# Score products of two attention mixers: low keys padded to 128 rows, and 64-row products moved behind the 128-row ones

## The chip, the cores and the metric

The kernel runs on one core of a Trainium2 chip (trn2). The metric is the device time of one execution in microseconds (us). Of the core's engines the text speaks of TensorE (PE: matrix products; its loads of the stationary operand have a row of their own, PEld), VectorE (DVE), ScalarE (ACT), GpSimd (POOL) and the queue that starts most transfers (SP). TensorE computes with a stationary operand that it loads first and a moving operand that it streams. The result goes to PSUM, from where DVE and ACT read it. A product "with 128 rows" contracts over all 128 partitions, one "with 64 rows" over half of them.

## The reference

A decoder trunk of two layers, sequence 512, width 1024. Each layer is a channel mixing (SwiGLU), a token mixer, and another channel mixing. The token mixer of layer 0 is a convolution beside sparse attention, that of layer 1 a short convolution beside stick-breaking attention. What the change touches are the scores, queries times keys, of eight heads of 64 in either mixer:

```python
def _nsa(q, kc, vc, ks, vs, kw, vw, gates, ...):          # layer 0
    ...
        s_s = jnp.einsum('bqgrd,bgqnd->bqgrn', qg, k_sel).astype(jnp.float32) * scale
        ...
        s_w = jnp.einsum('bqgrd,bsgd->bqgrs', qg, kwb).astype(jnp.float32) * scale
        ...
        o = gq[..., 0:1] * o_c + gq[..., 1:2] * o_s + gq[..., 2:3] * o_w

def _stick_breaking(q, k, v):                             # layer 1
    ...
        z = jnp.einsum('bqhd,bshd->bhqs', qb, k).astype(jnp.float32) * scale
        ...
        log_a = jax.nn.log_sigmoid(z) + lax.cumsum(log_keep, axis=3, reverse=True) - log_keep
```

In layer 0 the selected and the window branch both cover all earlier tokens here (sequence 512, window 512, all blocks selected), so that each head has two full causal score matrices.

## The kernel before

**Precision.** Every operand is kept as a high part and a low part (`split`, lines L93 and L94: ACT rounds, DVE subtracts), and a product is the sum of high times high, high times low and low times high. A head has 64 features, half of the 128 partitions. So a query tile holds the high part in one half of the partitions and the low part in the other half, and a key tile holds the high keys twice. One product with 128 rows then gives (high + low query) times high key. What is missing, high query times low key, is a second product with 64 rows that uses only the half with the high query.

**First mixer** (`mixer0`, layer 0). After the projections, L735 to L764 do the compressed branch. The loop over eight heads (in the order 0, 4, 1, 5, ...) and two branches follows: for four blocks `i` of 128 queries a score tile `ss` with (i+1)*128 columns is computed by L815 (128 rows, stationary `qst`, moving `kt_`) and L816 (64 rows, the same stationary columns, moving `klo`). DVE adds the bias and takes the extremum (L818), ACT takes the exponential (L820), POOL scales by the gate (L825), PE transposes (L487, ten blocks for one head and branch), ACT and DVE split what comes out (`th`, `tl`, L93 and L94), and PE weighs the values (L497, L498). At the end of a head L830 and L831 add the compressed branch (32 rows), and ACT and DVE join the halves (L477, L478). A convolution of one channel block runs on PE (`cv`, L123 to L125) and that of three others on DVE (`cc`, L559), both as filling work with a late priority. `klo` is two tiles, one for each branch: its lower 64 partitions belong to key group 0, its upper ones to key group 1.

**Second mixer** (`mixer1`, layer 1). For each of eight heads a tile `z` of three PSUM banks takes, for the blocks 3, 2, 0, 1, a product with 128 rows (L912), one with 64 rows (L913) and the causal mask as a product with the identity (L916, L919). Two sigmoids of ACT read the whole `z` (L922, L925), DVE makes the running product (L929, L930), then come transposes and weighing as in the first mixer. The projections of the short convolution (`ac`, L123 to L125, through `short_conv`) fill PE with a late priority. There is one `z` buffer.

**Order.** The instructions of each engine are put in a fixed order by a list scheduler when the program is built: by a priority that follows the order of the code, lowered for what stands under `later()`, and by its own estimate of times. On the chip each engine runs its list in order and waits by semaphores. Buffers are rotating pools; of the tags that matter here the first mixer has three `ss`, two `pt` and two `po` banks of PSUM.

Of the kernel before, what the change touches and what calls it, by code (L numbers as in the profile page):

```python
# [7 lines left out]
F32 = mybir.dt.float32  # L8
# [3 lines left out]
ALU = mybir.AluOpType  # L12
AX = mybir.AxisListType

P = 128
T = 512
# [14 lines left out]
OFFQ = [896, 1024, 512, 0]  # L31
# [24 lines left out]
def trunk(ctx: ExitStack, tc: tile.TileContext, a: dict, out: bass.AP):  # L56
    nc = tc.nc
    V, S, G, PE = nc.vector, nc.scalar, nc.gpsimd, nc.tensor
# [27 lines left out]
    ident_r = const.tile([P, P], F32R, name="ident_r")  # L86
    mask_r = const.tile([P, P], F32R, name="mask_r")
# [423 lines left out]
    def mixer0(norm, nxt, ph):  # L511
# [52 lines left out]
        qst = [qb[h // 3][:, (h % 3) * T:(h % 3 + 1) * T] for h in range(NH)]  # L564
# [107 lines left out]
        for n in (3, 3, 2):  # L672
            hi, lo = load_w(a["ab_v"][:, k * 280:(k + n) * 280], n * 280)
            for j in range(n):
                sl = slice(j * 280, (j + 1) * 280)
                for i in range(NT):
                    ts = slice(i * P, (i + 1) * P)
                    o = pvs[i][:, :280]
# [14 lines left out]

        kb = [ph.rtile("kst", "q", 1536) for _ in range(2)]
        kb = [b[:, i * T:(i + 1) * T] for b in kb for i in range(3)]
        kt_, klo = kb[:4], kb[4:]
        for br in range(2):
            pk = alt()
            proj(norm, a["ab_a"][10 + br], pk)
            kk = ctile("kk")  # L700
            V.tensor_tensor(kk, pk, rstd, ALU.mult)
            for g in range(2):
                r, r2 = slice(g * 64, g * 64 + 64), slice(64 - g * 64, 128 - g * 64)
                kg = kt_[2 * g + br]
                S.activation(kg[r, :], kk[r, :], AF.Copy)
                S.activation(kg[r2, :], kk[r, :], AF.Copy)
                V.tensor_tensor(klo[br][r, :], kk[r, :], kg[r, :], ALU.subtract)

        for j in range(4):
            pq = alt()  # L710
# [3 lines left out]
            for g in range(2):  # L714
                r, r2 = slice(g * 64, g * 64 + 64), slice(64 - g * 64, 128 - g * 64)
                q = qst[j + 4 * g]
# [55 lines left out]
        with later():  # L772
# [19 lines left out]
            for j in range(4):  # L792
                z = conv[j]
# [9 lines left out]
        for n, h in enumerate([0, 4, 1, 5, 2, 6, 3, 7]):  # L803
            g, hh, slope = h // 4, h % 4, 2.0 ** -(h + 1)
            rg = slice(g * 64, g * 64 + 64)
            po = pbt("po", "po")
            kw = dict(skip_group_check=True)
            for br in range(2):
                p_ = ph.tile("pp", "p", 1281)
                st = sm.tile([P, 8], F32, tag="st", name=nm("st"))  # L810
                for i in range(NT):
                    w = (i + 1) * P
                    ts = slice(i * P, (i + 1) * P)
                    ps = pbt("ss")
                    PE.matmul(ps[:, :w], qst[h][:, ts], kt_[2 * g + br][:, :w], start=True, stop=False)  # L815
                    PE.matmul(ps[:, :w], qst[h][rg, ts], klo[br][rg, :w], start=False, stop=True)  # L816
                    e = p_[:, OFFQ[i]:OFFQ[i] + w]
                    V.tensor_tensor_reduce(out=e, in0=ps[:, :w], in1=cst[:, C_U + T - w:C_U + T], scale=-slope,  # L818
                                           scalar=3e38, op0=ALU.add, op1=ALU.min, accum_out=st[:, i:i + 1])
                    S.activation(e, e, AF.Exp, scale=-1.0, bias=st[:, i:i + 1], accum_out=st[:, 4 + i:5 + i])  # L820
                V.reciprocal(st[:, 4:8], st[:, 4:8])
                V.tensor_tensor(st[:, 4:8], st[:, 4:8], gv[:, :, h, 1 + br], ALU.mult)
                for i in range(NT):
                    e = p_[:, OFFQ[i]:OFFQ[i] + (i + 1) * P]
                    G.tensor_scalar(e, e, st[:, 4 + i:5 + i], 1.0, op0=ALU.mult, op1=ALU.mult)  # L825
                th, tl = turned(p_, lambda s: pbt(s, "pt"), (lambda s: pbt(s, "cv")) if n >= 2 else None)
                weigh(po, th, tl, [vst[br][:, t, g] for t in range(NT)], br == 0, False)
            rows = slice(hh * NBLK, (hh + 1) * NBLK)
            vv = (vc0, vc1)[g][rows, :]
            PE.matmul(po, vv, pch[g][rows, :], start=False, stop=True, **kw)  # L830
            PE.matmul(po[:64, :], vv[:, :64], pcl[g][rows, :], start=False, stop=True, **kw)  # L831

            if g == 0:
                of = ctile("of")
            join(of[rg, :], po)
            if g == 1:
                split(o_h[hh], o_l[hh], of)
# [8 lines left out]
    def mixer1(norm, nxt, ph):  # L846
# [3 lines left out]
        qs, kh, kl = qk[:NH], qk[NH:2 * NH], qk[2 * NH:]  # L850
        for j in range(8):
            ps = ph.bank()
            proj(norm, a["cd_a"][12 + j], ps)
            t = ctile("qk")
# [50 lines left out]
        for h in range(NH):  # L905
            j, r = h // 2, slice((h % 2) * 64, (h % 2) * 64 + 64)
            z = ph.banks3("z").rearrange("p a b -> p (a b)")
            for i in (3, 2, 0, 1):
                w = (i + 1) * P
                o, ts = z[:, OFFQ[i]:OFFQ[i] + w], slice(i * P, w)  # L910
                kw = dict(skip_group_check=True)
                PE.matmul(o, qs[h][:, ts], kh[h][:, :w], start=i != 0, stop=False, **kw)  # L912
                PE.matmul(o, qs[h][r, ts], kl[j][r, :w], start=False, stop=False, **kw)  # L913

                if i == 0:
                    PE.matmul(z[:, OFFQ[2] + 2 * P:OFFQ[0] + P], ident_r, mask_r.unsqueeze(1).to_broadcast([P, 2, P]),  # L916
                              start=False, stop=True, **kw)
                elif i != 2:
                    PE.matmul(o[:, i * P:], ident_r, mask_r, start=False, stop=True, **kw)  # L919
            za = z[:, :1280]  # L920
            al = ph.tile("al", "p", 1281)
            S.activation(al[:, :1280], za, AF.Sigmoid)  # L922
            keep = ph.tile("keep", "p", 1281)
            V.memset(keep[:, 1280:], 1.0)
            S.activation(keep[:, :1280], za, AF.Sigmoid, scale=-1.0)  # L925

            for i in range(NT):
                x = keep[:, OFFQ[i] + 1:OFFQ[i] + (i + 1) * P][:, ::-1]
                V.tensor_tensor_scan(x, x, x, 1.0, ALU.mult, ALU.min)  # L929
            V.tensor_tensor(al[:, :1280], al[:, :1280], keep[:, 1:], ALU.mult)  # L930
            th, tl = turned(al, lambda s: ph.bank(s, "pt"))
            for _ in range(FILL[h]):
                short_conv()
            po = ph.bank("po")
            weigh(po, th, tl, [vst[t][:, h] for t in range(NT)], True, True)
            if h % 2 == 0:
                of = ctile("of")
            join(of[r, :], po)

            if h % 2 == 1:  # L940
                split(qs[h - 1], qs[h], of)
# [14 lines left out]
    with ffn_phase() as ph:  # L956
# [22 lines left out]
        V.tensor_copy(mask_r, mask)  # L979
        n1.finish(lambda s: ph.bank(s, "n"))  # L980
        ffn(n1, a["w1_in"][0], a["w1_out"][0], n2.add, ph, w_dir=a["w_dir"])
    with Phase(dict(q=6, t=5, p=3, d=4, cc=3), "p", "ss", ss=3, pt=2, po=2, cv=1) as ph:
        n2.finish(lambda s: ph.bank(s, "po"))
        mixer0(n2, n3.add, ph)
    with ffn_phase() as ph:
# [151 lines left out]
```

## Time and profile before

| | |
|---|---|
| time, median of 3 runs (lowest to highest) | 1969.65 us (1969.51 to 1969.8) |
| the profiled execution | 1969.98 us, of which its span is 1968.2 us |
| PE busy, matmuls | 1916.4 us, 97% of the span, 11862 matmuls |
| DVE busy | 1416.9 us, 72% |
| ACT busy | 943.3 us, 48% |
| POOL busy | 174.7 us, 9% |
| mean granted clock of TensorE | 0.981 of full speed |

The attention of the first mixer lies at 489 to 608 us of the span, that of the second at 1439 to 1521 us. A matmul's recorded duration runs past the start of the next one, because matmuls are pipelined. So its cost is read from start to start: the time from the start of one matmul to the start of the next. An interval that is longer than the streamed columns need is a stall, even where PE counts as busy. In the timeline the columns are: start in us, duration in us, engine, line, operation, what is written and read, rows*columns of the stationary operand, shape of the moving operand, and how many instructions were merged.

### The profile page before, as it was taken

The numbers are of one execution on the slowest core, as the hardware profiler recorded it, in microseconds if no ns is written. First come the engines' busy times: TensorE is split into PE (matmuls) and PEld (weight loads), VectorE is DVE, ScalarE is ACT, GpSimd is POOL, SyncE is SP. The second block draws the span as 40 slices with busy tenths as digits, with TensorE's granted clock in tenths as the row PEclk, the third lists the DMA queues.
The fourth block names the chain that finished last, engine by engine and source line by source line (L and its number), as shares of the span: only waits on it lengthen the run. The fifth ranks groups of instructions, "written<-read, shape, count | busy, mean of one in ns | idle before, by whom it ended". The sixth has DMA issues, their size and how long they took to land.

```text
span 1968.2 us, 29331 instructions
## 1 busy us (share of the span) xinstructions
PE 1916.4 (97%) x11862; PEld 1700.9 (86%) x11862; DVE 1416.9 (72%) x1978; ACT 943.3 (48%) x1330; POOL 174.7 (9%) x196
## 2 busy tenths in 40 slices
PE   8899999989999899999999999999999989999998
PEld 7899998778667799999989999998877879999997
DVE  6877765599875787767687776765568768776663
ACT  5544443336675554434355444434545445444433
POOL 2000000100222200000020000001000110000001
PEclk9899999989989899999999999999999989999999
DMA  7366552332102376656526666523221446665622
GB/s 251 97 180 164 147 133 73 97 109 76 44 1 54 112 183 164 173 149 157 146 75 170 169 167 157 152 64 119 87 66 62 114 115 176 168 167 139 162 57 82
DMA packets 74584, 244.76 MB, mean 124 GB/s; under 512 B 8272, under 2 KB 8656, under 8 KB 74448
## 3 DMA queue, kind: packets, MB, share of 16 engines
q1 hardware_dynamic: 62208, 198.70, 32.3%
q0 software_dynamic: 12096, 44.05, 13.1%
q8 instruction: 93, 1.52, 0.3%
q14 instruction: 43, 0.35, 0.1%
q10 hardware_dynamic: 144, 0.14, 0.0%
HBM read 240.76 MB, written 2.10 MB: 123 GB/s over the span
## 4 chain that ended last, share of the span: by engine, by line
PE 63%; DVE 2%; ACT 1%; issue 0%; DMA 0%; DVEq 0%; SPq 0%; ACTq 0%
PE px L315 20%; PE pw L315 10%; PE fo L125 6%; PE fo L123 6%; PE fo L124 6%; PE py L315 5%; PE ac L123 2%; PE ac L124 2%; PE ac L125 2%; PE mo L123 1%; PE mo L125 1%; PE mo L124 1%; PE z L913 1%; DVE xl L94 0%; PE pt L487 0%
## 5 line engine op out<-in xcount | busy, mean ns | idle before, releaser
L315 PE MATMUL px<-xh,whi 128*128 128x256 f32 x1344 | 334.1, 285 | 10.3 <-ACT xh L93 6.4
L93 ACT ACTIVATE whi<-raw 128x768 fp32r<-128x768 f32 (+3 forms) x201 | 175.9, 876 | 349.6 <-issue 111.0
L315 PE MATMUL px<-xl,whi 128*128 128x256 f32 x1344 | 334.3, 285 | 1.2 <-DVE xl L94 1.2
L93 ACT ACTIVATE whi<-rb 128x1024 fp32r<-128x1024 f32 x168 | 178.1, 1060 | 306.6 <-PE fo L124 156.5
L123 PE MATMUL fo<-act,whi 128*128 128x512 f32 (+1 forms) x710 | 279.7, 394 | 0.0
L125 PE MATMUL fo<-act,wlo 128*128 128x512 f32 (+1 forms) x710 | 279.2, 393 | 0.0
L124 PE MATMUL fo<-act,whi 128*128 128x512 f32 (+1 forms) x710 | 278.8, 393 | 0.0
L315 PEld LDWEIGHTS px<-xh,whi 128*128 128x128 f32 x1344 | 260.2, 194 | 15.5 <-ACT xh L93 7.4
L315 PEld LDWEIGHTS px<-xl,whi 128*128 128x128 f32 x1344 | 260.5, 194 | 4.6 <-DVE xl L94 1.7
L94 DVE TENSOR_TENSOR wlo<-raw,whi 128x768 fp32r<-128x768 f32 (+3 forms) x201 | 202.9, 1011 | 35.1 <-ACT whi L93 30.2
L94 DVE TENSOR_TENSOR wlo<-rb,whi 128x1024 fp32r<-128x1024 f32 x168 | 204.8, 1219 | 9.8 <-ACT whi L93 8.8
L367 DVE SCALAR_TENSOR_TENSOR xT<-fo,xT 128x512 f32<-128x512 f32 x129 | 88.5, 686 | 153.2 <-PE fo L125 153.1
L315 PE MATMUL px<-xh,wlo 128*128 128x256 f32 x1344 | 191.6, 286 | 0.0
L294 POOL DMA_DIRECT2D ws<-in_w_in x84 | 73.6, 876 | 1189.1 <-DMA ws<-in_w_in 641.1
L315 PEld LDWEIGHTS px<-xh,wlo 128*128 128x128 f32 x1344 | 176.3, 195 | 0.0
L315 PE MATMUL pw<-xl,whi 128*128 128x256 f32 x672 | 165.3, 283 | 0.0
L315 PE MATMUL pw<-xh,whi 128*128 128x256 f32 x672 | 165.2, 283 | 0.0
L125 PEld LDWEIGHTS fo<-act,wlo 128*128 128x128 f32 x710 | 133.7, 188 | 30.4 <-DVE wlo L94 0.2
L124 PEld LDWEIGHTS fo<-act,whi 128*128 128x128 f32 x710 | 134.2, 189 | 26.9
L123 PEld LDWEIGHTS fo<-act,whi 128*128 128x128 f32 x710 | 134.3, 189 | 26.0
L94 DVE TENSOR_TENSOR wlo<-ws,whi 128x1024 fp32r<-128x1024 f32 x84 | 102.5, 1221 | 40.8 <-ACT whi L93 39.3
L315 PEld LDWEIGHTS pw<-xh,whi 128*128 128x128 f32 x672 | 129.2, 192 | 1.2
(328 smaller groups left out, 3765.7 us busy)
## 6 DMA issues: line engine op xcount, KB each, us to landing
rb<-in_w_in SPq DMA_DIRECT2D x126, 512.0 KB, 4.0
ws<-in_w_in SPq DMA_DIRECT2D x84, 512.0 KB, 3.6
ws<-in_w_in POOLq DMA_DIRECT2D x84, 512.0 KB, 7.3
raw<-in_w_out SPq DMA_DIRECT2D x97, 384.0 KB, 3.2
raw<-in_cd_a SPq DMA_DIRECT2D x20, 512.0 KB, 3.3
raw<-in_w_out SPq DMA_DIRECT2D x32, 256.0 KB, 2.7
raw<-in_ab_a SPq DMA_DIRECT2D x16, 512.0 KB, 3.7
raw<-in_ab_w_out SPq DMA_DIRECT2D x8, 512.0 KB, 3.3
```

The costliest lines, as they stand in the source:

```text
L93: S.activation(hi, src, AF.Copy)
L94: V.tensor_tensor(lo, src, hi, ALU.subtract)
L123: PE.matmul(o, wh, xh, start=start, stop=False, **kw)
L124: PE.matmul(o, wh, xl, start=False, stop=False, **kw)
L125: PE.matmul(o, wl, xh, start=False, stop=stop, **kw)
L294: G.dma_start(ws[i], w_in[s, BLOCKS.index(b2)], accum_op=ALU.add)
L315: PE.matmul(o[:, j * TH:(j + 1) * TH], w[:, sl], norm.ops[k][op][x], start=first and w is hi and k + j + x == 0, stop=w is lo and k == 3, ...
L367: V.scalar_tensor_tensor(xT[:, m, ts], o, -0.5, xT[:, m, ts], op0=ALU.mult, op1=ALU.add)
L913: PE.matmul(o, qs[h][r, ts], kl[j][r, :w], start=False, stop=False, **kw)
```

## The change

In the first mixer the low keys get a tile for each pair of key group and branch, four tiles instead of two. The new ones come from a new pool `kl` of the phase. The half that doesn't belong to the group is set to zero by POOL, and the second score product streams all 128 rows. The zeros meet the low part of the query and add nothing. In the second mixer the 64-row products keep their rows, but move behind the 128-row products and masks of their head. No product is added or left out.

```diff
-        kt_, klo = kb[:4], kb[4:]
+        kt_, klo = kb[:4], kb[4:] + [ph.rtile("kl", "kl", T) for _ in range(2)]
...
-                V.tensor_tensor(klo[br][r, :], kk[r, :], kg[r, :], ALU.subtract)
+
+                G.memset(klo[2 * g + br][r2, :].bitcast(F32), 0.0)
+                V.tensor_tensor(klo[2 * g + br][r, :], kk[r, :], kg[r, :], ALU.subtract)
...
-                    PE.matmul(ps[:, :w], qst[h][rg, ts], klo[br][rg, :w], start=False, stop=True)
+                    PE.matmul(ps[:, :w], qst[h][:, ts], klo[2 * g + br][:, :w], start=False, stop=True)
...
+            kw = dict(skip_group_check=True)
             for i in (3, 2, 0, 1):
                 w = (i + 1) * P
                 o, ts = z[:, OFFQ[i]:OFFQ[i] + w], slice(i * P, w)
-                kw = dict(skip_group_check=True)
                 PE.matmul(o, qs[h][:, ts], kh[h][:, :w], start=i != 0, stop=False, **kw)
-                PE.matmul(o, qs[h][r, ts], kl[j][r, :w], start=False, stop=False, **kw)
 
                 if i == 0:
                     PE.matmul(z[:, OFFQ[2] + 2 * P:OFFQ[0] + P], ident_r, mask_r.unsqueeze(1).to_broadcast([P, 2, P]),
-                              start=False, stop=True, **kw)
+                              start=False, stop=False, **kw)
                 elif i != 2:
-                    PE.matmul(o[:, i * P:], ident_r, mask_r, start=False, stop=True, **kw)
+                    PE.matmul(o[:, i * P:], ident_r, mask_r, start=False, stop=False, **kw)
+            for i in (3, 2, 0, 1):
+                w = (i + 1) * P
+                o, ts = z[:, OFFQ[i]:OFFQ[i] + w], slice(i * P, w)
+                PE.matmul(o, qs[h][r, ts], kl[j][r, :w], start=False, stop=True, **kw)
...
-    with Phase(dict(q=6, t=5, p=3, d=4, cc=3), "p", "ss", ss=3, pt=2, po=2, cv=1) as ph:
+    with Phase(dict(q=6, t=5, p=3, d=4, cc=3, kl=2), "p", "ss", ss=3, pt=2, po=2, cv=1) as ph:
```

How the instructions of an engine stand is shown by rows of line, operation, what is written and read, and shape of the result. The numbers belong to the buffers and differ between the two programs. Lines of the changed kernel lie 2 to 11 higher.

TensorE, first head of the second mixer, before:

```order
L912 MATMUL z_13736<-qk_13287,qk_13285 128x512
L913 MATMUL z_13736<-qk_13290,qk_13285 128x512
L919 MATMUL z_13736<-mask_r,ident_r 128x128
L912 MATMUL z_13736<-qk_13287,qk_13285 128x384
L913 MATMUL z_13736<-qk_13290,qk_13285 128x384
L912 MATMUL z_13736<-qk_13287,qk_13285 128x128
L913 MATMUL z_13736<-qk_13290,qk_13285 128x128
L916 MATMUL z_13736<-mask_r,ident_r 128x256
L912 MATMUL z_13736<-qk_13287,qk_13285 128x256
L913 MATMUL z_13736<-qk_13290,qk_13285 128x256
L919 MATMUL z_13736<-mask_r,ident_r 128x128
```

The same place now; L914, L924, L917 and L920 are what L912, L913, L916 and L919 were:

```order
L914 MATMUL z_13746<-qk_13297,qk_13295 128x512
L920 MATMUL z_13746<-mask_r,ident_r 128x128
L914 MATMUL z_13746<-qk_13297,qk_13295 128x384
L914 MATMUL z_13746<-qk_13297,qk_13295 128x128
L917 MATMUL z_13746<-mask_r,ident_r 128x256
L914 MATMUL z_13746<-qk_13297,qk_13295 128x256
L920 MATMUL z_13746<-mask_r,ident_r 128x128
L924 MATMUL z_13746<-qk_13300,qk_13295 128x512
L924 MATMUL z_13746<-qk_13300,qk_13295 128x384
L924 MATMUL z_13746<-qk_13300,qk_13295 128x128
L924 MATMUL z_13746<-qk_13300,qk_13295 128x256
```

Four separate 64-row products have become one run of four. In other heads the scheduler puts other 128-row products into the run, as in the sixth head, again on TensorE (L487 is a transpose):

```order
L924 MATMUL z_14297<-qk_13301,qk_13296 128x512
L924 MATMUL z_14297<-qk_13301,qk_13296 128x384
L487 MATMUL pt_14120<-cst,al_14094 128x128
L487 MATMUL pt_14120<-cst,al_14094 128x128
L924 MATMUL z_14297<-qk_13301,qk_13296 128x128
L924 MATMUL z_14297<-qk_13301,qk_13296 128x256
```

So this head has two runs of two. Over the eight heads the 32 products stand in 11 runs: 4, 4, 3, 1, 4, 4, 2, 2, 4, 1, 3.

POOL, between the last transfers that it starts for the channel mixing ahead of the first mixer (L294) and the sums of squares of that mixer's norm (L205), before:

```order
L294 DMA ws_2859<-in_w_in 128x1024
L205 TENSOR_TENSOR ss_3318<-sq_3285,sq_3316 128x512
```

and now:

```order
L294 DMA ws_2859<-in_w_in 128x1024
L708 MEMSET kl_4254 64x512
L708 MEMSET kl_4255 64x512
L205 TENSOR_TENSOR ss_3318<-sq_3285,sq_3316 128x512
```

Two of the four memsets stand ahead of the sums of squares; the other two stand behind the last of these and ahead of the first scaling of the scores. The list of SP is the same in both programs. In the first mixer PE's list is the same up to the fifth head; from there on some score products, transposes and weighings have changed places by a few rows.

## Rows read from the trace of the kernel before

**Rows 1.** The chain that ended last, 480 to 720 us: its first piece.

```profile
661.88 1.43 issue
```

**Rows 2.** Timeline of PE in the first mixer: start, duration, line, tiles, shapes, count.

```profile
502.52 0.40 PE L815 MATMUL ss<-kst,qst 128*128 128x512 f32 x1
502.85 0.49 PE L816 MATMUL ss<-kst,qst 64*128 64x512 f32 x1
503.27 0.72 PE L735 MATMUL sc<-qst,keep 128*128 128x512 f32 x2
503.83 0.22 PE L815 MATMUL ss<-kst,qst 128*128 128x128 f32 x1
503.98 0.32 PE L816 MATMUL ss<-kst,qst 64*128 64x128 f32 x1
504.24 0.49 PE L125 MATMUL cv<-cx,wlo 128*128 128x504 f32 x1
504.57 0.39 PE L123 MATMUL cv<-cx,whi 128*128 128x504 f32 x1
504.80 0.39 PE L124 MATMUL cv<-cx,whi 128*128 128x504 f32 x1
```

**Rows 3.** Line L816's instructions: count, duration ns min/median/max, first and last start.

```profile
L816 PE MATMUL ss<-kst,qst x64: 322/436/792, 489.5 to 607.7; 64*128 64x128 f32 x16, 64*128 64x256 f32 x16, 64*128 64x384 f32 x16, 64*128 64x512 f32 x16
```

**Rows 4.** Stretches: busy us of PE, PEld, DVE, ACT, POOL; clock, DMA share, GB/s.

```profile
489.00:546.00 57.00, 55.70 (x253) 39.42 (x252) 51.15 (x127) 40.42 (x109) 14.02 (x22) 1.00 0.12 38
546.00:558.00 12.00, 12.00 (x51) 8.41 (x51) 7.10 (x29) 5.35 (x14) 4.10 (x8) 0.72 0.01 1
558.00:570.00 12.00, 9.64 (x38) 6.12 (x37) 10.08 (x25) 11.90 (x27) 0.00 (x0) 0.72 0.00 1
570.00:576.00 6.00, 5.47 (x24) 3.21 (x23) 3.17 (x14) 3.20 (x10) 2.05 (x4) 0.99 0.00 1
576.00:608.00 32.00, 32.00 (x162) 21.30 (x161) 24.58 (x86) 26.10 (x76) 12.74 (x24) 1.00 0.00 1
...
1436.00:1546.00 110.00, 110.00 (x524) 84.93 (x523) 90.92 (x131) 54.64 (x70) 0.00 (x0) 1.00 0.19 61
```

**Rows 5.** Waits of DVE, then of ACT, 489 to 608: total us, times, longest.

```profile
DVE pp L818 <- PE pt L487: 5.5, 6, 1.9
DVE pp L818 <- PE ss L816: 5.4, 6, 1.5
DVE th L94 <- ACT th L93: 3.9, 6, 1.2
...
ACT th L93 <- PE pt L487: 16.4, 13, 2.6
```

**Rows 6.** Timeline of PE, second head of the second mixer: its first product, and the second behind it.

```profile
1448.12 0.39 PE L912 MATMUL z<-qk,qk 128*128 128x512 f32 x1
...
1451.42 0.39 PE L124 MATMUL ac<-xn,whi 128*128 128x512 f32 x1
```

**Rows 7.** Timeline of PE at a head's end in the first mixer.

```profile
554.82 0.49 PE L830 MATMUL po<-pc,keep 32*128 32x512 f32 x1
555.15 0.38 PE L831 MATMUL po<-pc,keep 32*64 32x512 f32 x1
```

**Rows 8.** Timeline of PE ahead of 546 us, and the stretch behind it.

```profile
544.31 1.72 PE L223 MATMUL rs<-ones,lq 128*128 128x1 f32 x14
...
546.00:550.00 4.00, 4.00 (x16) 2.77 (x15) 2.30 (x11) 0.60 (x1) 2.05 (x4) 0.52 0.00 0
```

**Rows 9.** Timelines of DVE and POOL (in brackets idle time before), and SP's wait.

```profile
307.18 1.23 DVE L94 TENSOR_TENSOR wlo<-ws,whi 128x1024 fp32r<-128x1024 f32 x1 [1.40 <-ACT whi L93]
...
345.67 1.42 POOL L205 TENSOR_TENSOR ss<-sq,sq 128x512 f32<-128x512 f32 x1 [71.49 <-ACT sq L200]
...
502.14 2.85 POOL L825 TENSOR_SCALAR pp<-pp,st 128x128 f32<-128x128 f32 x4 [133.66 <-ACT whi L540]
...
SPq L293 <- DVE al L94: 88.7, 1, 88.7
```

## Prediction

> **What bounds the kernel now.** First the chain that ended last: between 480 and 720 us its first piece starts at 661.88 us [rows 1]. So it says nothing of the two attention stretches, at 489 to 608 us and 1439 to 1521 us, and these have to be read from the timeline, the stretches and the waits. In the table of stretches PE counts as busy nearly throughout in the first mixer and for all of 110 us in the second, while DVE is busy for 90% and 77% in the longest two stretches of the first mixer (51.15 of 57.00, 24.58 of 32.00) and 83% in the second (90.92 of 110) [rows 4]. But busy isn't streaming, as the timeline shows. A plain 128-row matmul of 504 columns starts 0.23 us before the next one (504.57 to 504.80), that is 0.456 ns for a column [rows 2].
>
> Around a 64-row product the starts lie further apart. The pair with 512 columns: 0.33 us from L815 to L816 (0.10 over plain), then 0.42 us to the next product (0.19 over), and the two L735 behind it take 0.56 us instead of 0.46 (0.10 over). Together 0.39 us. The pair with 128 columns and the product behind it: 503.83 to 504.57 is 0.74 us for 128+128+504 = 760 columns, which at 0.456 ns are 0.35 us; 0.39 us over [rows 2]. So whatever its width, a 64-row product that stands alone among 128-row ones costs about **0.39 us of PE beyond its columns**, and this sits inside what counts as busy. In the second mixer the 11 products of a head and the first one behind it take 3.30 us (1448.12 to 1451.42) [rows 6] for 1280+1280+512+512 = 3584 columns, 1.63 us; 1.67 us over, 0.42 for each of four.
>
> **The change part by part.**
>
> *First mixer, PE.* All 64 second products [rows 3] get 128 rows, stream the same columns, and stand alone no more: 64 x 0.39 = 25.0 us. Something comes back. A matmul can't start sooner than about 0.11 us after one with other weights, even with a single column: 14 of them take 1.72 us with the tail of the last [rows 8]. A 128-column product streams for 0.06 us, so that 32 such products (16 pairs) pay 0.05 each, 1.6 us. PE is relieved of **23.4 us**.
>
> *How much of that reaches the end.* From 489 to 608 us DVE is busy for 51.15+7.10+10.08+3.17+24.58 = 96.1 of 119 us [rows 4]. Its work stays the same, so the stretch can't shrink by more than 22.9 us. DVE waits directly for transposes and scores of PE for 5.5+5.4 = 10.9 us, and 3.9 us for ACT, which itself waits 16.4 us for PE's transposes [rows 5]. From 558 to 570 us ACT is busy for 11.90 of 12 us, so that a faster PE gives nothing there [rows 4]. I take the direct waits and half of those through ACT, 10.9+1.9 = **13 us**. The bounds are half of the direct waits, 5.5 us (DVE and ACT, at 77% and 82% from 576 to 608, wait for each other instead), and 22.9 us (DVE never waits). 13 is nearer to the middle, since DVE already runs at 90% from 489 to 546 with its taps as filling work and has little to give there, while from 546 to 608 it idles over a quarter of the time.
>
> *Memsets on POOL.* Four, 128x512 at half the partitions. The trace has no memset of this kind; the nearest rows are POOL's scalings, 2.85 us for four of 128 to 512 columns, and a sum of 1.42 us [rows 9]. So between 0.3 and 1.5 us each. Two stand ahead of the norm's sums, in POOL's 71.49 us of idle time before 345.67; they wait for the tiles of the channel mixing whose memory they take, whose last reader is DVE until 308.4 us, which leaves 37 us for at most 3 us [rows 9]. The other two stand in the 133.66 us of idle time before 502.14 [rows 9]. Cost 0. Without that cover the norm's sums queued behind them would be late by up to 3 us. The subtractions of the low keys are four as before. The SP queue is unchanged. Its first transfer into that memory for the next channel mixing waits 88.7 us, for the last split of the convolution's result [rows 9], which comes after all uses of the new tiles, so that these hold nothing up.
>
> *Second mixer, PE.* The 32 lone products become 11 runs. If a run pays for one way in and one way out, 21 x 0.39 = 8.2 us go. In a head two masks and two products are 128 columns wide and now stand at the floor of 0.11 us, 4 x 0.05 x 8 = 1.6 us back: **6.6 us** of PE. No wait of PE shows in 1436 to 1546 us, since the projections fill it, so nearly all should pass. DVE would go from 83% to 90.92 of 103.4, 88%, a share at which it still waits for PE in the first mixer. I take 6 us; bounds 4 (DVE's waits move to PE, as the scheduler fixed its order without these stalls' relief in view) and 6.6. The sigmoids start when the whole `z` is done, before and after, and `z` is done sooner.
>
> *Sum.* 13 + 6 = 19 us, against the profiled execution 1969.98 - 19 = **1951 us**; this execution lies 0.3 us over the median, which changes nothing. What follows either stretch (output projection, norm, channel mixing) keeps its own length and moves forward as a whole. Bounds: 9.5 us (1960.5) to 29.5 us (1940.5).
>
> [...] The second product of a head's compressed branch follows the first one on the same 32 rows: L830 to L831 is 0.33 us at 512 columns, 0.10 over plain [rows 7]. L830 has just been switched to, and 0.10 is what a product right behind a switch pays anyway [rows 2]. So L831's own load costs nothing more, and a run of 64-row products should stream at plain pace.
> [...]
>
> **The rivals.**
>
> 1. *DVE and ACT take over.* In the first mixer they wait for each other where they waited for PE; in the second DVE is the bound. Gains 5.5 and 4 us: 1960.5 us. For it: the shares above, ACT's 11.90 of 12. Against it: the 10.9 us are waits for PE alone.
> 2. *Everything passes*, up to DVE's work: 22.9 and 6.6 us, 1940.5 us. For it: the half of the waits that I left out hangs on PE by one step more. Against it: three engines with three `ss` banks and two `pt` banks between them seldom reach 100%.
> 3. *The loads in a run are exposed.* Of 21 products that follow a 64-row one each pays the 0.11 us of a load that isn't hidden, 2.3 us: the second mixer gives 4 us, 1953 us.
> 4. *The stall isn't made by the number of rows.* The second product writes the same columns of `ss` as the first and has the same weights' columns. Were that the cause, full rows would change nothing, and the gain of the second mixer could go with it: 1970 us. Against it: L123 to L125 also add into one tile one after the other, at 0.23 us [rows 2].
> [...]
>
> **How the numbers follow.** Forecast 0.53 (1946 to 1956 us), rival 1 0.22, rival 2 0.10, rival 3 0.06, rival 4 0.05, rival 5 0.04. The forecast, rivals 1, 2 and 3 are faster by more than 0.2% (3.9 us, about what a measurement of this kernel can tell from no change): 0.91. Rival 4 is the same, 0.05; rival 5 slower, 0.04. For 8 in 10 the range takes in the forecast, rival 3, rival 1 as far as 1961 and the nearer part of rival 2: 1942 to 1961 us.
>
> **What would show it.** In the timeline of the changed kernel the second score product of a pair with 512 columns should start 0.23 us after the first, and the one behind it again 0.23 us later. In the second mixer a whole run of four should cost about 0.4 us beyond its columns, not 1.7. The stretch from the first to the last score product of the first mixer should go from 119 to about 106 us, with DVE's waits for PE a few us and its busy share near 90%; that of the second mixer up to the end of its output projection from 107 to about 101 us. I'm wrong if the pairs keep their 0.3 to 0.4 us; if the pairs are plain but the first mixer's stretch stays near 114 us (rival 1: the waits then stand between DVE, ACT and POOL); or if the granted clock falls below 1.00 in stretches where it was full.

## The result, and the profile after

| | before | after |
|---|---|---|
| time, median (lowest to highest), runs side by side | 1969.72 us (1969.51 to 1970.03) | 1941.54 us (1940.73 to 1942.76) |
| span of the profiled execution | 1968.2 us | 1939.7 us |
| mean granted clock of TensorE | 0.981 | 0.985 |

The changed kernel takes 0.9861 of the time before, 95% interval 0.9849 to 0.9872: 28.2 us less, where 19 were forecast. Both stretches gave more than their term: the first mixer, from its first to its last score product, 118.4 to 102.1 us, 16.3 less (forecast 13); the second, from its first score product to its last `ac` projection, 108.2 to 100.0 us, 8.2 less (forecast 6). The other 4.0 us of the span lie where nothing is changed: 0.9 ahead of the first score product, 0.7 between the two stretches, 2.4 behind the second.

The stretches are read from groups of lines (count, duration in ns min/median/max, first and last start, shapes). In the kernel before, beside [rows 3], these give the first score product, and the first `z` and the last `ac` of the second mixer:

```profile
L815 PE MATMUL ss<-kst,qst x64: 219/374/797, 489.3 to 607.3; 128*128 128x128 f32 x16, 128*128 128x256 f32 x16, 128*128 128x384 f32 x16, 128*128 128x512 f32 x16
...
L912 PE MATMUL z<-qk,qk x32: 278/358/481, 1439.6 to 1519.8; 128*128 128x512 f32 x8, 128*128 128x384 f32 x8, 128*128 128x128 f32 x8, 128*128 128x256 f32 x8
...
L125 PE MATMUL ac<-xn,wlo x123: 387/389/478, 1399.9 to 1547.8; 128*128 128x512 f32 x123
```

These are the changed kernel's score products in the first mixer, then `ac` and `z` in the second:

```profile
L817 PE MATMUL ss<-kst,qst x64: 218/364/796, 488.4 to 590.2; 128*128 128x128 f32 x16, 128*128 128x256 f32 x16, 128*128 128x384 f32 x16, 128*128 128x512 f32 x16
L818 PE MATMUL ss<-kst,qst x32: 272/312/632, 488.5 to 581.1; 128*128 128x128 f32 x8, 128*128 128x256 f32 x8, 128*128 128x384 f32 x8, 128*128 128x512 f32 x8
L818 PE MATMUL ss<-kl,qst x32: 272/333/416, 502.2 to 590.5; 128*128 128x128 f32 x8, 128*128 128x256 f32 x8, 128*128 128x384 f32 x8, 128*128 128x512 f32 x8
...
L125 PE MATMUL ac<-xn,wlo x97: 387/389/504, 1399.7 to 1521.7; 128*128 128x512 f32 x97
...
L914 PE MATMUL z<-qk,qk x32: 221/334/478, 1421.7 to 1495.4; 128*128 128x512 f32 x8, 128*128 128x384 f32 x8, 128*128 128x128 f32 x8, 128*128 128x256 f32 x8
```

All 64 products of L818 have 128 rows. The timeline of PE at the place of [rows 2] (start, duration, line, tiles, shapes, count):

```profile
501.25 0.40 PE L817 MATMUL ss<-kst,qst 128*128 128x512 f32 x1
501.49 0.39 PE L818 MATMUL ss<-kst,qst 128*128 128x512 f32 x1
501.71 0.63 PE L737 MATMUL sc<-qst,keep 128*128 128x512 f32 x2
502.18 0.22 PE L817 MATMUL ss<-kst,qst 128*128 128x128 f32 x1
502.24 0.27 PE L818 MATMUL ss<-kl,qst 128*128 128x128 f32 x1
502.35 0.44 PE L125 MATMUL cv<-cx,wlo 128*128 128x504 f32 x1
502.63 0.39 PE L123 MATMUL cv<-cx,whi 128*128 128x504 f32 x1
```

512 columns: 0.24 and 0.22 us from start to start, where [rows 2] had 0.33 and 0.42. The narrow pair with the product behind it takes 0.45 us (502.18 to 502.63) instead of 0.74. Plain would be 0.35: the last 128-column product and the wide one behind it pay 0.05 each.

The second head of the second mixer, answering to [rows 6]:

```profile
1430.51 0.39 PE L914 MATMUL z<-qk,qk 128*128 128x512 f32 x1
...
1431.37 0.22 PE L920 MATMUL z<-mask_r,ident_r 128*128 128x128 f32 x1
1431.52 0.91 PE L924 MATMUL z<-qk,qk 64*128 64x512 f32 x4
1432.36 0.50 PE L123 MATMUL ac<-xn,whi 128*128 128x512 f32 x1
1432.69 0.40 PE L124 MATMUL ac<-xn,whi 128*128 128x512 f32 x1
```

From 1430.51 to 1432.69 are 2.18 us, 3.30 before. The same timeline in narrower windows shows the starts inside the run, by how many of the four are left:

```profile
1431.86 0.57 PE L924 MATMUL z<-qk,qk 64*128 64x384 f32 x3
...
1432.04 0.39 PE L924 MATMUL z<-qk,qk 64*128 64x128 f32 x2
...
1432.10 0.33 PE L924 MATMUL z<-qk,qk 64*128 64x256 f32 x1
```

The way in: the mask ahead of the run takes 0.15 us (0.09 over plain) and the 512 columns 0.34 (0.11 over). Inside, 384 take 0.18 and 128 take 0.06 (both plain). The way out: 256 take 0.26 up to the first 128-row product (0.14 over), and that product 0.33 (0.10 over). Together they are about 0.45 us for a run of four, where the prediction had 0.39 for a run and the price of narrow products apart.

The waits of DVE for PE and ACT, of PE for DVE, then of ACT, from 488 to 600 us (total us, times, longest), answering to [rows 5]:

```profile
DVE pp L820 <- PE pt L487: 1.6, 1, 1.6
DVE th L94 <- ACT th L93: 1.4, 4, 0.6
DVE pp L820 <- PE ss L818: 0.4, 1, 0.4
...
PE ss L817 <- DVE st L820: 2.1, 4, 0.8
...
ACT th L93 <- PE pt L487: 6.6, 11, 1.1
```

DVE's direct waits for PE fell from 10.9 to 2.0 us, and PE now waits for DVE's reading of a score bank. The stretches (busy us of PE, PEld, DVE, ACT, POOL, each with its count of instructions; then clock, DMA share, GB/s), first mixer as a whole, a piece of it, and the second mixer:

```profile
488.00:590.50 102.50, 93.84 (x522) 73.79 (x521) 96.98 (x280) 86.10 (x232) 34.30 (x59) 0.98 0.07 21
...
562.00:566.00 4.00, 3.62 (x15) 3.29 (x16) 2.99 (x13) 3.13 (x10) 1.85 (x4) 0.57 0.01 2
...
1418.00:1528.00 110.00, 110.00 (x561) 90.82 (x560) 95.79 (x138) 57.48 (x74) 0.00 (x0) 1.00 0.21 70
```

DVE is busy for 96.98 of 102.5 us, 95%, where [rows 4] gives 96.1 of 119, 81%: the same work with 5.5 us of idle time instead of 22.9. The granted clock is 0.57 for one piece of 4 us, where [rows 4] has a mean of 0.72 over 24 us. In the second mixer PE has no idle time, as before.

### The profile page after: what moved, and what is told of

It reads as the page before. It is cut to its first block, busy times and chain, and to the rows that moved or that the text cites. A ratio compares the mean times of both kernels' runs of the same rounds, so it can differ in the third digit from the quotient of the medians.

```text
span 1939.7 us, 29340 instructions
## 1 busy us (share of the span) xinstructions
PE 1884.6 (97%) x11862; PEld 1693.8 (87%) x11862; DVE 1415.4 (73%) x1978; ACT 942.4 (49%) x1330; POOL 178.5 (9%) x200
## 4 chain that ended last, share of the span: by engine, by line
PE 63%; DVE 2%; ACT 1%; issue 0%; DMA 0%; DVEq 0%; ACTq 0%; SPq 0%
PE px L315 20%; PE pw L315 10%; PE fo L125 6%; PE fo L123 6%; PE fo L124 6%; PE py L315 5%; PE ac L125 2%; PE ac L123 2%; PE ac L124 2%; PE mo L123 1%; PE mo L124 1%; PE mo L125 1%; DVE xl L94 1%; PE pt L487 0%; DMA rb<-in_w_in 0%
## 5 line engine op out<-in xcount | busy, mean ns | idle before, releaser
L315 PE MATMUL px<-xh,whi 128*128 128x256 f32 x1344 | 334.1, 285 | 10.9 <-ACT xh L93 6.4
L94 DVE TENSOR_TENSOR wlo<-raw,whi 128x768 fp32r<-128x768 f32 (+3 forms) x201 | 202.5, 1009 | 34.7 <-ACT whi L93 29.7
L294 POOL DMA_DIRECT2D ws<-in_w_in x84 | 73.6, 876 | 1181.7 <-DMA ws<-in_w_in 532.7
```

Of the source, the lines that this page charges most:

```text
L94: V.tensor_tensor(lo, src, hi, ALU.subtract)
L294: G.dma_start(ws[i], w_in[s, BLOCKS.index(b2)], accum_op=ALU.add)
L315: PE.matmul(o[:, j * TH:(j + 1) * TH], w[:, sl], norm.ops[k][op][x], start=first and w is hi and k + j + x == 0, stop=w is lo and k == 3, ...
```

## The experiments

Beside these kernels the kernel before took 1969.0 us (1963.75 to 1970.82) in the first set of runs (the first four kernels below), 1969.04 (1963.27 to 1984.1) in the second (`before_taps21`, `after_taps21`, `after_pool`, `pad1`) and 1969.13 (1964.09 to 1970.16) in the third (`half0`, `nolow0`, `pad1_pool`), whose expectations were written with the results of the second known. Ratios are to the kernel before of the same set. Differences from the changed kernel go across sets. Stretches and clocks below are those of one profiled execution of each kernel; "score stretch" is the time from the first to the last score product of the first mixer.

**The first mixer alone** (`m0_only`): the changed kernel with the old order in the second mixer.

```diff
                 PE.matmul(o, qs[h][:, ts], kh[h][:, :w], start=i != 0, stop=False, **kw)
+                PE.matmul(o, qs[h][r, ts], kl[j][r, :w], start=False, stop=False, **kw)
...
-            for i in (3, 2, 0, 1):
-                w = (i + 1) * P
-                o, ts = z[:, OFFQ[i]:OFFQ[i] + w], slice(i * P, w)
-                PE.matmul(o, qs[h][r, ts], kl[j][r, :w], start=False, stop=True, **kw)
```

> Only the first mixer's part of the change (zero-padded low keys, all score products with 128 rows); the second mixer as before. Theory (each lone 64-row product costs 0.39 us of PE, DVE becomes the bound of the first mixer): 17 us less than before, about 1952.5 us, as the traces' shift of 17 us at the first product of the next channel mixing says; the second mixer's stretch keeps its 107 us. Rival (part of the 28 us comes from the two parts together, or from a different start of the run): the two single parts don't add up to 28 us, this one gives 13 us or less.

1949.59 us (1948.07 to 1950.25), ratio 0.9901 (0.9887 to 0.9914): 19.4 us faster, 2.4 more than expected. The second mixer's stretch keeps its length (1421.6 to 1529.4, 107.8 us, 108.2 before).

**The second mixer alone** (`m1_only`): the kernel before with the same lines the other way round.

> Only the second mixer's part (64-row products of a head behind its 128-row ones); the first mixer as before. Theory: 21 of 32 stalls of 0.39 to 0.42 us go, PE is never waited out there, so 8.2 to 9.5 us less than before, 1960 to 1961.5 us. Rival of the prediction (narrow products pay a floor of 0.11 us each, and DVE takes part of the gain): 6 us less, 1964 us.

1958.42 us (1956.81 to 1960.47), ratio 0.9947 (0.9935 to 0.9959): 10.6 us faster. First score product of that mixer to last `ac`: 99.6 us, 8.6 less than before, inside the expected 8.2 to 9.5; the whole lies 1.1 us above it. The parts add up to 30.0 us against 28.2 together, so neither needs the other.

**The norm's sums, before and after** (`before_rs128`, `after_rs128`). The 16 one-column sums ahead of the clock's first fall [rows 8] are made 128 columns wide.

```diff
-    def rsqrt_rows(bank, parts, scale, eps, col, row):
+    def rsqrt_rows(bank, parts, scale, eps, col, row, n_=1):
...
-                PE.matmul(ps[:, j:j + 1], p_[:, j * P:(j + 1) * P], ones[:, 0:1],
+                PE.matmul(ps[:, j * n_:(j + 1) * n_], p_[:, j * P:(j + 1) * P], ones[:, :n_],
...
-        V.tensor_scalar(v, ps[:, :nt], scale, eps, op0=ALU.mult, op1=ALU.add)
+        V.tensor_scalar(v, ps[:, :nt * n_:n_], scale, eps, op0=ALU.mult, op1=ALU.add)
...
-            rsqrt_rows(lambda s: pbt(s, "cv"), sqs, 1.0 / T, LN_EPS, lc, rstd)
+            rsqrt_rows(lambda s: pbt(s, "cv"), sqs, 1.0 / T, LN_EPS, lc, rstd, P)
```

> The kernel before, with the 16 one-column sums of the layer norm in the first mixer made 128 columns wide (each column the same sum; DVE reads one of them). [...] Theory that part of the first mixer's 17 us is TensorE's clock: the fall of the granted clock to 0.5 at 546 to 553 us goes away, and the time falls by 3 to 5 us to about 1966 us. Rival (the fall comes from something else, or costs nothing since DVE and ACT are waited for anyway): clock falls as before, or the time stays within 1 us of 1969.7.

> The changed kernel with the same wide sums. In its trace the clock is full at 536 to 550 us already, so by the clock theory nothing is left to gain there: 1941.5 us within 1 us, and the one fall at 562 to 566 us, which follows ACT's stretch, stays. Rival (wide sums are quicker or slower by themselves): the time moves by over 1 us with the clock unchanged.

Before: 1968.03 us (1960.59 to 1969.13), ratio 0.9986 (0.9975 to 0.9996): 1.0 us faster, not the 3 to 5 of the theory. After: 1939.87 us (1938.26 to 1940.87), ratio 0.9852 (0.9838 to 0.9865), 1.7 us under the changed kernel, more than the 1 us expected, while in the trace the fall has grown from 4 to 11 us (560 to 571 us at 0.54), as in `m0_only`; its time is won between the mixers (591.9 to 1420.8 us, 2.3 less than after), where nothing is changed. The stretches of `before_rs128` where the kernel before has its falls, and then of `m0_only`:

```profile
546.00:553.00 7.00, 7.00 (x38) 4.52 (x36) 5.51 (x24) 4.90 (x13) 3.15 (x7) 1.00 0.01 2
558.00:566.00 8.00, 6.85 (x20) 4.51 (x20) 6.57 (x20) 8.00 (x19) 0.00 (x0) 0.57 0.00 0
```

```profile
560.00:571.00 11.00, 9.88 (x38) 8.04 (x37) 6.34 (x25) 7.33 (x23) 6.15 (x12) 0.54 0.00 1
```

The 16 sums themselves take hardly longer with 128 columns: from the first start to the last 4.5 us (540.6 to 545.1), with one column 4.4 (541.4 to 545.8). In this execution of `before_rs128` the first fall is gone and the score stretch is 115.3 us, 3.1 shorter than before. `m0_only` has the same list of PE in the first mixer as the changed kernel, but 11 us at 0.54 where that has 4 us at 0.57, and its score stretch is 104.3 us, 2.2 longer. So a longer or a further fall costs two to three us here, and which falls come differs between kernels with equal lists. The sums aren't the whole reason: the changed kernel issues the same 14 one-column products and keeps the clock at 1.00 behind them. What decides it stays open.

```profile
538.95 1.67 PE L223 MATMUL rs<-ones,lq 128*128 128x1 f32 x14
...
542.00:546.00 4.00, 3.81 (x23) 2.73 (x21) 4.00 (x15) 2.86 (x10) 1.57 (x3) 1.00 0.00 0
```

The falls inside the score stretch, read from such rows, lie beside its length as follows. "Lost" is the length of a fall times what its clock lacks to 1.00; it is an estimate of what PE loses if it never waits.

| | score stretch | falls: us at mean granted clock | lost, at most |
|---|---|---|---|
| before | 118.4 us | 7 at 0.51, 8 at 0.58 | 6.8 us |
| `before_rs128` | 115.3 | 8 at 0.57 | 3.4 |
| `half0` | 107.2 | 8 at 0.57 | 3.4 |
| after | 102.1 | 4 at 0.57 | 1.7 |
| `m0_only` | 104.3 | 11 at 0.54 | 5.1 |
| `after_rs128` | 104.1 | 11 at 0.54 | 5.1 |
| `after_pool` | 100.0 | none | 0 |

**Half of the padding** (`half0`): the selected branch back at 64 rows.

```diff
-                    PE.matmul(ps[:, :w], qst[h][:, ts], klo[2 * g + br][:, :w], start=False, stop=True)
+                    rk = rg if br == 0 else slice(0, P)
+                    PE.matmul(ps[:, :w], qst[h][rk, ts], klo[2 * g + br][rk, :w], start=False, stop=True)
```

> The changed kernel with the second score product of the selected branch (32 of the 64 of the first mixer) back at 64 rows; the window branch keeps 128. PE gets back 32 x 0.39 = 12.5 us of stall. Theory (in the changed kernel PE, DVE and ACT take turns in waiting for each other, so that the second half of the relief was worth less than the first): 2 to 6 us slower than the changed kernel, 1943.5 to 1947.5 us. Rival (PE sets the pace at every point between, so that the 17 us of the first mixer divide evenly): 8 to 9 us slower, 1949.5 to 1950.5 us.

1945.74 us (1944.88 to 1946.14), ratio 0.989 (0.9873 to 0.9907): 4.2 us slower than the changed kernel. The score stretch runs from 489.6 to 596.8 us:

```profile
L817 PE MATMUL ss<-kst,qst x64: 219/364/797, 489.6 to 596.5; 128*128 128x128 f32 x16, 128*128 128x256 f32 x16, 128*128 128x384 f32 x16, 128*128 128x512 f32 x16
...
L819 PE MATMUL ss<-kl,qst x32: 274/359/628, 503.5 to 596.8; 64*128 64x128 f32 x4, 64*128 64x256 f32 x4, 64*128 64x384 f32 x4, 64*128 64x512 f32 x4
```

118.4, 107.2, 102.1 us with none, half and all of the lone products gone: the first 12.5 us of PE's stalls were worth 11.2 us, the second 12.5 us 5.1. Part of this is clock: before has one fall more than `half0`, worth 3.1 us by `before_rs128`, and `half0` a longer one than after. Without the 3.1 the first half is worth 8.1 us. The relief fades, as the theory had it, but less than the two numbers say.

**Less work for DVE, before and after** (`before_taps21`, `after_taps21`).

```diff
-            for s in range(CW):
+            for s in range(CW - 10):
```

> The kernel before, with the last 10 of the 31 taps of the convolution of three channel blocks left out on DVE (the output is not the reference's). This takes 30 DVE instructions of about 0.70 us, 21 us of DVE's work, out of the first mixer. Theory (before the change PE's stalled score products set the pace of the heads, DVE has 23 us of idle time from 489 to 608 us): 0 to 4 us faster than the kernel before, 1965 to 1970 us. Rival (DVE set the pace already, and the change worked by something else): 8 us faster or more, below 1962 us.

> The changed kernel with the same 10 taps left out (the output is not the reference's), 21 us less of DVE's work. Theory (DVE is busy for 94.6% from the first to the last score product and is now the bound): 8 to 12 us faster than the changed kernel, 1930 to 1934 us, with the two waits of PE for DVE's reading of the scores shorter. Rival (PE or ACT is still the bound): 0 to 4 us, 1937.5 to 1941.5 us.

Before: 1965.44 us (1962.34 to 1967.64), ratio 0.9977 (0.9958 to 0.9996), 3.6 us faster, as expected; its score stretch is 117.7 us, 0.7 shorter, with 20 us at 0.57 in three falls. After: 1937.59 us (1936.27 to 1938.26), ratio 0.9847 (0.9832 to 0.9861), only 4.0 us faster than the changed kernel, where 8 to 12 were expected. The stretch from its start to the last score product:

```profile
488.00:586.50 98.50, 92.89 (x522) 74.80 (x520) 81.53 (x253) 84.55 (x231) 31.88 (x58) 0.97 0.06 22
```

DVE's share has dropped to 83%: its work here is 15.5 us less (81.53 against 96.98). Yet the score stretch is only 4.2 us shorter (97.9 us). Two falls of the clock, 6 us at 0.72 each, stand where the changed kernel has one of 4 us; they hide 1.7 us more at most. So my theory that DVE at 95% is *the* bound falls. That ACT (86%) or PE (94%) takes over is likely, but not shown.

**Less work for PE** (`nolow0`): without the second score products of the first mixer.

```diff
-                    PE.matmul(ps[:, :w], qst[h][:, ts], kt_[2 * g + br][:, :w], start=True, stop=False)
-                    PE.matmul(ps[:, :w], qst[h][:, ts], klo[2 * g + br][:, :w], start=False, stop=True)
+                    PE.matmul(ps[:, :w], qst[h][:, ts], kt_[2 * g + br][:, :w], start=True, stop=True)
```

> The changed kernel without the second score products of the first mixer: the product of high query and low key is left out (the output is not the reference's). It takes 64 products of 320 columns in the mean, 20480 x 0.456 ns = 9.3 us of streaming, from PE and nothing from DVE or ACT. Theory (no engine alone is the bound any more): 1 to 4 us faster than the changed kernel, 1937.5 to 1940.5 us. Rival (PE still sets the pace): 8 to 9 us faster, 1932.5 to 1933.5 us.

1936.41 us (1935.39 to 1938.19), ratio 0.9844 (0.9827 to 0.9862): 5.1 us faster than the changed kernel, between the two expectations. The profiled execution is the longest of the four, 3.3 us shorter than that of the changed kernel. Only 0.8 of this lies in the score stretch (101.3 us), where the clock falls twice; most of the rest lies between the mixers, where nothing is changed:

```profile
530.00:536.00 6.00, 5.14 (x20) 3.25 (x19) 5.38 (x13) 3.27 (x8) 5.00 (x8) 0.72 0.01 3
550.00:560.00 10.00, 7.52 (x27) 5.78 (x27) 9.69 (x27) 10.00 (x25) 0.00 (x0) 0.66 0.01 2
```

From 550 to 560 us ACT works without a gap, PE idles for a quarter of the time, and the granted clock goes to a mean of 0.66. These falls take 5.1 us at most from PE, 3.4 more than that of the changed kernel, so that at an equal clock the stretch could be up to 4.2 us shorter instead of 0.8. That the idler PE makes the fall isn't shown: the next kernel has much the same piece at full clock.

**Eight operations from DVE to POOL** (`after_pool`).

```diff
-                V.tensor_tensor(z, z, rstd, ALU.mult)
+                G.tensor_tensor(z, z, rstd, ALU.mult)
...
-            split(a_h[j], a_l[j], conv[j])
+            S.activation(a_h[j], conv[j], AF.Copy)
+            G.tensor_tensor(a_l[j], conv[j], a_h[j], ALU.subtract)
```

> The changed kernel with eight operations of DVE in the first mixer given to POOL: the four products with the norm's factor after the convolution and the four low parts of its result, 8 x 0.69 = 5.5 us of DVE. Theory (DVE is the bound of the first mixer): 2 to 5 us faster, 1936.5 to 1939.5 us. Rival (POOL's scalings of the probabilities queue behind the moved work, and the heads wait for these): no gain, or up to 3 us slower, 1941.5 to 1944.5 us.

1939.98 us (1938.91 to 1941.92), ratio 0.9861 (0.9846 to 0.9875): 1.6 us under the changed kernel, with runs that overlap. Inconclusive. Two things moved at once in the trace: DVE's work in the score stretch fell by 2.1 of the 5.5 us (96.58 to 94.46), and the clock stayed full, also where ACT works without a gap and PE idles:

```profile
556.00:570.00 14.00, 11.34 (x66) 8.02 (x64) 11.37 (x39) 13.95 (x40) 6.03 (x11) 1.00 0.00 1
```

**Padding in the second mixer too** (`pad1`).

```diff
-                    V.tensor_tensor(kl[j - 4][r, :], t[r, :], x[r, :], ALU.subtract)
+                    lo = kl[2 * (j - 4) + g]
+                    G.memset(lo[r2, :].bitcast(F32), 0.0)
+                    V.tensor_tensor(lo[r, :], t[r, :], x[r, :], ALU.subtract)
...
-                PE.matmul(o, qs[h][r, ts], kl[j][r, :w], start=False, stop=True, **kw)
+                PE.matmul(o, qs[h][:, ts], kl[h][:, :w], start=False, stop=True, **kw)
```

> The changed kernel with the low keys of the second mixer padded by zeros too, one tile for each head, so that all its score products have 128 rows and the 11 runs of 64-row products are gone. Theory (every run still costs about 0.4 us beyond its columns, PE bounds this stretch): 11 x 0.39 = 4.3 us less PE, some 4 us faster, about 1937.5 us. Rival (DVE, busy for 95.8 of 110 us, takes it): 0 to 1 us, 1940.5 to 1941.5 us.

1935.85 us (1935.36 to 1937.28), ratio 0.984 (0.9825 to 0.9854): 5.7 us faster than the changed kernel, and the fastest that computes everything. The second head and the ends of the stretch:

```profile
1428.04 0.39 PE L918 MATMUL z<-qk,qk 128*128 128x512 f32 x1
...
1428.97 0.87 PE L928 MATMUL z<-qk,qk 128*128 128x512 f32 x4
1429.67 0.40 PE L123 MATMUL ac<-xn,whi 128*128 128x512 f32 x1
1429.90 0.40 PE L124 MATMUL ac<-xn,whi 128*128 128x512 f32 x1
```

```profile
L125 PE MATMUL ac<-xn,wlo x96: 387/389/481, 1421.7 to 1515.6; 128*128 128x512 f32 x96
...
L918 PE MATMUL z<-qk,qk x32: 221/335/479, 1419.6 to 1490.1; 128*128 128x512 f32 x8, 128*128 128x384 f32 x8, 128*128 128x128 f32 x8, 128*128 128x256 f32 x8
```

The head takes 1.86 us (2.18 with a run), and the stretch 96.0 us, 4.0 less than after: 0.36 for each of the 11 runs, where 0.39 was expected. Most of the rest of the 5.7 us isn't the padding's: between the mixers the same list of PE gains 1.5 us on that of the changed kernel from 1009 to 1016 us, where the granted clock differs (from 1010 to 1020 us a mean of 0.87 here and 0.69 there).

**Both** (`pad1_pool`).

> The kernel with the low keys of the second mixer padded too, and with the eight operations of the first mixer given from DVE to POOL. Theory (one edit takes stalls from PE in the second mixer, the other work from DVE in the first; they add): 5.7 + 1.6 us faster than the changed kernel, about 1934 us. Rival (what the second edit gave was the scatter of the runs): 1935.9 us, as with the padding alone.

1936.87 us (1933.63 to 1938.2), ratio 0.9842 (0.9819 to 0.9864): no faster than the padding alone, as the rival had it. The move to POOL gave nothing that can be measured.

## Why the prediction was right in its steps and short in its size

*The price of a lone 64-row product held.* Pairs are plain (0.24 and 0.22 us for 512 columns), a run of four pays about 0.45 us for one way in and one way out, and `pad1` takes away 0.36 us with each run. In the first mixer the relief can be sized over all intervals: each interval between two starts of PE with different numbers of rows, less its columns at 0.444 ns (0.227 us for 512, the pace of the `ac` products from 454.8 to 487.7 us in the changed kernel), and of that at most 0.2 us. The sum is 23.8 us before, 12.4 in `half0` and 1.1 after, a relief of 22.7 against the forecast 23.4. This is a check of the size only: the sorting leaves out the 0.10 us on the product behind a lone one, and takes in a part of other waits. The stretch shrank by 16.3; PE stood idle for 8.7 us of it after (102.50 less 93.84), for 4.2 before [rows 4].
In the traces it is the change of the number of rows that costs: 0.39 us for the way in and out of a lone product, while inside the run the products take 0.18 us for 384 columns and 0.06 for 128, no more than their columns. What takes the time in the change, no run shows.

*First mixer, 13 us forecast, 16.3 measured: the step "how much of that reaches the end" had no term for the clock.* Of the waits that the term counted, DVE's direct ones went from 10.9 to 2.0 us and those for ACT from 3.9 to 1.4: 11.4 us. I had taken all of the first and half of the second, 13 in all; this is near, though ACT's own waits for PE's transposes, which fell from 16.4 to 6.6 us, may have carried more. The clock is what I left out: its falls in the stretch lost 6.8 us at most before and 1.7 after. By `before_rs128` (3.4 us less lost, 3.1 us shorter) and `m0_only` (3.4 us more lost, 2.2 us longer) these 5.1 us are worth some 3 to 5. At an equal clock the first mixer gives about 11 to 13 us, so that the forecast 13 was about met. What the 16.3 has above it is the clock: luck, or an effect of the change on the clock. Which of the two, no run shows.
The repeated executions say the same of the whole. Beside the experiments the kernel before ran 35 times: four executions with a mean granted clock of 0.985 or 0.986 took 1963.3 to 1964.3 us, seven at 0.983 took 1965.6 to 1968.6, those from 0.980 to 0.982 took 1968.5 to 1970.8, and one at 0.973 took 1984.1. The four of the changed kernel, 1940.7 to 1942.8 us, had 0.984 or 0.985. So at an equal clock the change gives about 22 us, and some 6 of the 28.2 go with the clock.
DVE ended at 95%, above the 90% that I named, but `after_taps21` and `nolow0` show no single engine at the bound: 15.5 us less on DVE in the stretch give 4.0, and 9.3 us less on PE give 5.1.

*Second mixer, 6 us forecast, 8.2 measured: the step of the floor was mis-sized.* I counted 21 x 0.39 = 8.2 us and took off 1.6 for narrow products at a floor of 0.11 us and 0.6 for DVE. In the second head 3 x 0.39 = 1.17 us should have gone, less 0.2 for the floor; 1.12 went. The floor of 0.11 us holds for the one-column products of [rows 8], but not for 128 columns: such a product takes 0.06 us (502.18 to 502.24), and the one behind it takes 0.05 longer. About half of these 0.05 us were in the kernel before too, in the 0.42 for each of four that I had read from [rows 6]. So about half of the 1.6 was taken off twice. DVE took nothing either: 95.79 of 110 us busy, and PE without a gap. What I called the end of the output projection in the list of signs is the end of `ac`, at 1548 us before; the output projection follows it.

*The memsets cost nothing*, as forecast: two at 0.52 us each stand in POOL's idle time,

```profile
300.92 0.98 POOL L708 MEMSET kl<- 64x512 f32 x2 [27.69 <-DVE wlo L94]
```

inside the bounds of 0.3 to 1.5 us, ahead of any sum that could queue behind them: the first starts at 344.78 us. The other two, at 367.6 us, follow the last sum. The first two didn't wait for the last reader that I had named, until 308.4 us, but for an earlier split of DVE.

*The rivals.* Rival 1 (1960.5) falls: DVE and ACT did come near, but only after most of the relief had passed. Rival 2 (1940.5) has the time nearest to the result, but in part by the clock. Its first half is close (17.4 us of DVE's 22.9 of idle time went), its second half is not what happened, since 8.2 us are more than the 6.6 that it allowed. I gave it 0.10 with the remark that three engines seldom reach 100%; DVE reached 95%, ACT 84% (86.10 of 102.5). Rival 3 falls on the 0.18 and 0.06 us inside the run, which are the time of 384 and 128 columns alone. Rival 4 falls on the plain pairs: they write the same columns of `ss` as before. Rival 5, the slower one at 0.04, falls with the time. Of falls of the clock, too, there were fewer in the score stretch: one of 4 us at 0.57 against 7 at 0.51 and 8 at 0.58 before. `nolow0`, whose PE has less to do, has longer ones again (means of 0.72 over 6 us and 0.66 over 10), but `after_pool` none, so that no run shows an idler PE to be the cause.

## What to carry to other kernels

A lone 64-row matmul among 128-row ones cost a way in and a way out here, 0.39 us with 128 columns as with 512 [rows 2], and a profile that counts PE as busy hides it: read starts, not shares. Padding by zeros removed it at no cost in streaming (0.24 and 0.22 us for 512 columns, start to start), and putting such products in a row left about 0.45 us for a run of four; where memory allowed it, padding won (`pad1` against the runs: 4.0 us in the stretch). What a relief of PE was worth fell as DVE and ACT came near (11.2, then 5.1 us for two equal halves, some 3 us of the first by the clock), so that the waits of the others, the indirect ones too, gave a better size (13 us) than PE's own relief (23.4). Where executions of one kernel differ in their granted clock, compare times at an equal clock: here that is 22 us instead of 28.

## What the runs showed of the hardware

- The 0.39 us of a lone 64-row product splits into 0.10 on the product ahead of it, 0.19 on itself and 0.10 on the one behind [rows 2]. A run of four has 0.09 ahead, 0.11 on the first, 0.14 on the last and 0.10 behind. Some 0.1 of these 0.45 us belongs to narrow products, as with full rows the same head is only 0.32 shorter. Inside the run 384 columns take 0.18 us and 128 take 0.06, no more than their columns at the 0.456 ns of [rows 2].
- In the second head of `pad1`, behind a 128-column product, 384 and 128 columns take 0.29 us (1428.33 to 1428.62), 0.06 more than their columns at 0.456 ns. In the changed kernel the wide product behind a 128-column one took 0.28 us for 504 columns (502.35 to 502.63), 0.05 over plain.

```profile
1428.28 0.22 PE L924 MATMUL z<-mask_r,ident_r 128*128 128x128 f32 x1
1428.33 0.45 PE L918 MATMUL z<-qk,qk 128*128 128x384 f32 x2
1428.62 0.33 PE L921 MATMUL z<-mask_r,ident_r 128*128 128x256 f32 x1
```

- TensorE's granted clock differs between executions of equal lists of PE: 11 us at 0.54 or 4 us at 0.57 in the same place, 2.2 us apart in the stretch. Over a whole execution of the kernel before, a mean of 0.980 goes with 1968.5 to 1970.6 us, and one of 0.986 with 1963.3 to 1964.3 us.
